# Two token halves of an HGRN head stepped together, each with its own PSUM bank

## The chip, the cores and the metric

The kernel runs on one core of a Trainium2 chip. The metric is device time in microseconds (us) of one execution. Engine names are those of the profile: PE is TensorE's matmul, DVE is VectorE, ACT is ScalarE, POOL is GpSimd, SP issues the DMAs. Each engine has its own list of instructions, and semaphores order the lists against each other.

## The reference, cut to what matters

One layer over 2048 tokens of width 1024. A combined projection gives the inputs of a pooling branch and of an HGRN branch (a gated linear recurrence of 8 heads, 128 wide). For each head the kernel must give

```
cum   = cumsum(logf)                       # within a chunk
score[t,s] = sum_d q[t,d] k[s,d] exp(cum[t,d]-cum[s,d])   for s <= t
o     = (q*exp(cum)) @ state + score @ v
state = exp(last) * state + (k*exp(last-cum))^T @ v
o     = rms_norm(o) * g * silu(gate)
```

followed by two output projections, gates and a final projection with a norm.

## The kernel before, in words

The 2048 tokens go through in two passes of 1024, and a pass in two halves of T = 512 tokens (t = 0, 1), a half being NT = 4 chunks of 128 or NB = 16 blocks of 32 tokens. After the V projection (`v_job`) a pass runs a stage over its 8 heads, then the projections `psA`, `psB` and `psy`.

In the head stage a head has three `quad`s (L470): "fq", "m" and "gp" (for the last head "gp" comes before "m"). A quad is seven products in Strassen's manner, each of 12 matmuls of 128x512 (`three`, L279), over four PSUM banks named `pa`, `pb`, `pe`, `pd` with the quad's name behind them (`pam`, `pem`, `pdm`, `pbm` belong to "m"). The order of the products in a quad is: `pa`; `pe`; `pa` again; `pb`; `pa` a third time; `pe` again; `pd`. Ahead of the last one stands `A.copy(d, a)` (L497), which ACT does from `pa` after its third product, while PE does `pe`; the `pd` product adds onto what the copy put there.

Between the products `tick()` (L961) gives each active generator one step. `hgrn` (L523) is such a generator, one for a head and a half. Its steps:

- `QR`, `K`, `TT`: operands built on ACT and DVE;
- four rounds of scores. Three of them, from `QR`, `X2` and `X8` (named so in the kernel's tiles), are 16 matmuls of 32 weight columns and 48 moving columns (`scores`, L597), into PSUM tile `psa`. After each, DVE writes the valid ones into `PT` with `copy_predicated` (`put`, L565: 2 after the first, 3 after each of the others) and updates `K` (`kup`, L555). The fourth round, called s64 below, has 16 matmuls of 32 or 64 columns (L648 to L653), and three ACT copies empty it;
- `pk` (transposes of K, copied to `KS` by ACT), `pd` (L671), the states `SC` (L676, DVE, four in a chain that starts from `S[h]`), `po` (16 profile records, L682), then `A.copy(S[h], ...)`, four squares `junk` on ACT (L688), two small operations on POOL (L689, L690), four scaled copies `on` on ACT (L693), and the transposes `pot` (L699).

Steps of the generator are apart by `yield`s, three between rounds of scores. Every fp32 matmul is two records in the profile, so a score round of 16 shows as x32.

`psa` is one tile of two banks, with 64 columns for each of the 16 blocks; a block's 32 rows stand in its own quarter of the partitions. Both halves of a head, and the next head, use it in turn. The second half's generator starts after the first of the two later quads, so seven ticks behind the first half. Four score buffers' worth of `qr` tiles are shared, and tag `px` has two banks for `pk`, `pd`, `po`, `pot`, `pw` and `xT`.

What stands where on an engine is not the order of the code: the tile framework places the instructions of every engine in a fixed list when the program is built, by its own costs, and the hardware keeps to these lists.

Of the kernel before, what the change touches and what calls it, by code (L numbers as in the profile page):

```python
# [8 lines left out]
F32 = mybir.dt.float32  # L9
# [9 lines left out]
P = 128  # L19
SEQ = 2048  # L20
D = 1024
T = 512
NT = T // P
NB = T // 32
# [8 lines left out]
LOOK = 4  # L33
MASK_W = P + 2 * 64 + 5 * NT * 64
NU = 76
KINDS = (("m", "gp"), ("gp", "m"))


# [30 lines left out]
def tile_block(ctx: ExitStack, tc: tile.TileContext, x, c, w_ada, b_ada, g_pre, g_post, w_in,  # L69
# [3 lines left out]
    V, A, G, PE, SP = nc.vector, nc.scalar, nc.gpsimd, nc.tensor, nc.sync  # L73
# [13 lines left out]
    ph = ctx.enter_context(tc.tile_pool(name="ph", bufs=1, space=bass.MemoryType.PSUM))  # L87
# [30 lines left out]
    r0 = 0  # L118
# [7 lines left out]
    mask = cst.tile([P, MASK_W], U8, name="mask")  # L126
# [43 lines left out]
    def split(src32, hi, lo):  # L170
        return A.copy(hi, src32), V.tensor_tensor(lo, src32, hi.bitcast(F32), op=SUB)  # L171
# [104 lines left out]
    def mm(o, l, r, start, stop):  # L276
        PE.matmul(o, lhsT=l, rhs=r, start=start, stop=stop, skip_group_check=True)  # L277
# [13 lines left out]
        return pj.tile([P, T], F32, tag="pj", name=name)  # L291


    psa = ph.tile([P, 2 * T], F32, tag="ph", name="psa")
    V.memset(psa, 0.0)
    s48 = psa.rearrange("p (b w) -> p b w", w=64)
    shv = cst.tile([P, 8], F32, name="shv")
    scv = cst.tile([P, 8], F32, name="scv")

# [28 lines left out]

    def ada_done(q):
        acc = accs.pop(q)  # L330
        v = psa[:, T + q * 4:T + q * 4 + 4]
        for j in range(4):
            it = PE.matmul(v[:, j:j + 1], lhsT=acc[:, j * P:(j + 1) * P], rhs=one, start=True, stop=True)
        sl = slice(q * 2, q * 2 + 2)
        V.tensor_tensor(shv[:, sl], v[:, 0:2], col("bsh")[:, sl], op=ADD)
        V.tensor_tensor(scv[:, sl], v[:, 2:4], col("bsc")[:, sl], op=ADD)
        iv = V.scalar_tensor_tensor(scv[:, sl], scv[:, sl], 1.0, col("gpre")[:, sl], op0=ADD, op1=MUL)
        return it, iv
# [171 lines left out]
    gens = [0]  # L510
# [12 lines left out]
    def hgrn(p, h, t, cx):  # L523
        n = f"{p}_{h}_{t}"
        F, Q = cx["F"].pop((h, t)), cx["Q"].pop((h, t))
# [4 lines left out]
        K = utile("K" + n)  # L530
# [5 lines left out]
        o = 0  # L536
        for hh in (1, 2, 4, 8, 16, 32, 64):
            w = T // (2 * hh)
            a = v2(Tb[hh], 2)
# [3 lines left out]
        yield  # L543

        pt = PT[gens[0] % 2]
        gens[0] += 1
        vh = cx["V"][h]

# [14 lines left out]
        moff = [0]  # L563

        def put(dst, src):  # L565
            shp = list(dst.shape[1:])
            w = int(np.prod(shp))
            if len(shp) == 2:
                w = w // NT
                m = mask[:, moff[0]:moff[0] + w].rearrange("p (a b) -> p a b", b=shp[1])  # L570
                m = m.unsqueeze(1).broadcast_to([P, NT, w // shp[1], shp[1]])
                dst = dst.rearrange("p (c a) b -> p c a b", c=NT)
                src = src.rearrange("p (c a) b -> p c a b", c=NT)
            else:
                m = mask[:, moff[0]:moff[0] + w]
                m = m.rearrange("p (a b c) -> p a b c", b=shp[1], c=shp[2])
                src = src.rearrange("p a (b c) -> p a b c", c=shp[2])
            V.copy_predicated(dst, m, src)  # L578
            moff[0] += w

        def blk(ap, b, hh):

# [14 lines left out]
        def scores(X):  # L597
            for i in range(NB):
                r0 = (i % 4) * 32
                mm(s48[r0:r0 + 32, i, 0:48], K[:, i * 32:(i + 1) * 32], X[:, i, :], True, True)  # L600

        def build(hh, b, w):
            X = qp.tile([P, b, 3 * w], F32, tag="qr", name=f"X{hh}_{n}")
# [16 lines left out]
        put(blk(ptf, NB, 1), s48[:, :, 32:48])  # L620
        kup(1)
        X = build(2, NB, 16)
        yield
        yield
        yield
        for hh in (2, 8):
            scores(X)
            put(blk(ptf, NB, hh), s48[:, :, 0:16])
            put(blk(ptf, NB, 2 * hh), s48[:, :, 16:32])
            put(blk(ptf, NB, 2 * hh), s48[:, :, 32:48])  # L630
            kup(hh)
            kup(2 * hh)
            if hh == 2:
                X = build(8, NB, 16)
            else:
                X = qp.tile([P, T], F32, tag="qr", name=f"X32_{n}")
                x32 = X[:, 0:T // 2].rearrange("p (b w) -> p b w", w=32)
                A.copy(x32, blk(Q, NB // 2, 32))
                qup(32)
                x64 = X[:, T // 2:T].rearrange("p (b w) -> p b w", w=64)  # L640
                tq = Tb[32].rearrange("p (a b) -> p a b", b=4)
                q64 = blk(Q, NT, 64)
                tt(x64, q64, bc(tq[:, :, 1], 64))
            yield
            yield
            yield
        s64 = psa.rearrange("p (c w) -> p c w", c=NT)
        for cc in range(NT):  # L648
            o = cc * P
            mm(s64[0:32, cc, 0:32], K[:, o:o + 32], x32[:, 2 * cc, :], True, True)  # L650
            mm(s64[32:64, cc, 64:128], K[:, o + 32:o + 64], Q[:, o + 64:o + P], True, True)
            mm(s64[64:96, cc, 0:32], K[:, o + 64:o + 96], x32[:, 2 * cc + 1, :], True, True)
            mm(s64[0:32, cc, 64:128], K[:, o:o + 32], x64[:, cc, :], True, True)  # L653
        A.copy(pt[0:64, :, 64:128], s64[0:64, :, 64:128])
        A.copy(pt[0:32, :, 32:64], s64[0:32, :, 0:32])
        A.copy(pt[64:96, :, 96:128], s64[64:96, :, 0:32])
        kup(32)
# [48 lines left out]
    def pv_got(p, g, t, u, cx):  # L706
        n = f"{p}_{g}_{t}"
        w = WINDOWS[g]
        PV = qp.tile([P, HALO + T], F32, tag="qr", name="PV" + n)
        A.copy(PV[:, 0:HALO], halo[:, g, :])  # L710
        A.copy(PV[:, HALO:], u)
        A.copy(halo[:, g, :], PV[:, T:T + HALO])
        cur, lo = PV, 0
        sh = 1
        while sh < w:
            nx = qp.tile([P, HALO + T], F32, tag="qr", name=f"W{sh}_{n}")
            lo += sh
            tt(nx[:, lo:], cur[:, lo:], cur[:, lo - sh:HALO + T - sh], op=ADD)
            cur = nx
            sh *= 2  # L720
        pm = utile("pm" + n)
        V.scalar_tensor_tensor(pm, cur[:, HALO:], 1.0 / w, PV[:, HALO:], op0=MUL, op1=SUB)
        if p == 0 and t == 0:
            e0 = pm[:, 0:HALO]
            tt(e0, cur[:, HALO:2 * HALO], icnt[:, g * HALO:(g + 1) * HALO])
            tt(e0, e0, PV[:, HALO:2 * HALO], op=SUB)
        pmh, pml = utile("pmh" + n, F32R), utile("pml" + n, F32R)
        split(pm, pmh, pml)
        yield
        pw = px.tile([P, T], F32, tag="px", name="pw" + n)  # L730
        wh, wl = pwh[:, g * P:(g + 1) * P], pwl[:, g * P:(g + 1) * P]
        mm(pw, wh, pmh, True, False)
        mm(pw, wh, pml, False, False)
        mm(pw, wl, pmh, False, True)
        pws = utile("pws" + n)
        A.activation(pws, pw, AF.Copy, scale=col("psc", g))
        cx["pw"][g, t] = pws
        yield
# [181 lines left out]
    for p in range(NPASS):  # L920
        cx = {k: {} for k in ("sm", "F", "Q", "G", "V", "pw", "Gd", "Pd", "Sd", "gP", "gG", "a", "mg", "x", "xc", "h32",
                              "mv", "y", "yss")}
# [13 lines left out]
    for p in range(NPASS):  # L936
# [4 lines left out]
        for h in range(NH):  # L941
            quad_items(("fq", h), O_F + h * P, O_Q + h * P, p == 0)
            for kind in KINDS[h == NH - 1]:
                if kind == "m":
# [14 lines left out]
    active = []  # L959
# [45 lines left out]
    for p in range(NPASS):  # L1005
        cx = cxs[p]
# [33 lines left out]
        for h in range(NH):  # L1040
            if h + 1 < NH:
                v_head(p, h + 1, cx)
            n = f"{p}_{h}"

            def fq(row, t, u):
                (f_got, q_got)[row](p, h, t, u, cx)

            def gp(row, t, u):
                if row == 1:
                    g_got(p, h, t, u, cx)  # L1050
                elif h % 2 == 1:
                    pg_got(p, h // 2, t, u, cx)
                else:
                    gen = pv_got(p, h // 2, t, u, cx)
                    next(gen)
                    active.append(gen)

            steps = []

            def tick_in():  # L1060
                tick()
                once(steps)

            quad("fq" + n, cx, fq, tick)
            active.append(hgrn(p, h, 0, cx))
            tick()
            for i, kind in enumerate(KINDS[h == NH - 1]):
                if kind == "gp":
                    quad("gp" + n, cx, gp, tick)
                else:  # L1070
                    if h == NH - 1:
                        steps += [lambda: None] * 2
                        steps += [lambda g=g: two_in("P", p, g, cx) for g in range(NG - 1)]
                    quad("m" + n, cx, lambda row, t, u: m_got(p, h, row, t, u, cx), tick_in)
                if i == 0:
                    active.append(hgrn(p, h, 1, cx))
                tick()
            if p + 1 < NPASS:
                x_stats(8 + h)
# [57 lines left out]
```

## Time and profile before

| | |
|---|---|
| median of 3 runs | 1841.29 us (1841.15 to 1844.52) |
| the profiled execution | 1843.0 us, span 1841.2 us |
| PE busy | 1797.7 us of the span |
| DVE busy | 1103.1 us |
| ACT busy | 807.5 us |
| head stage, first pass | from about 160 us to 700 us |
| head stage, second pass | from about 1030 us to 1600 us |

A busy time counts the union of an engine's instructions. In the chain of waits a row is a start, a duration, an engine, and a group of instructions that follow each other without a break; "x12" are profile records. Since the chain's pieces of PE follow each other without gaps, the duration of a piece is what it takes of PE's time, which is less than the duration of its instructions, as these overlap.

### The profile page before, as it was taken

The numbers are of one execution on the slowest core, as the hardware profiler recorded it, in microseconds if no ns is written. First come the engines' busy times: TensorE is split into PE (matmuls) and PEld (weight loads), VectorE is DVE, ScalarE is ACT, GpSimd is POOL, SyncE is SP. The second block draws the span as 40 slices with busy tenths as digits, with TensorE's granted clock in tenths as the row PEclk, the third lists the DMA queues.
The fourth block names the chain that finished last, engine by engine and source line by source line (L and its number), as shares of the span: only waits on it lengthen the run. The fifth ranks groups of instructions, "written<-read, shape, count | busy, mean of one in ns | idle before, by whom it ended". The sixth has DMA issues, their size and how long they took to land.

```text
span 1841.2 us, 31695 instructions
## 1 busy us (share of the span) xinstructions
PE 1797.7 (98%) x12053; PEld 1458.0 (79%) x12053; DVE 1103.1 (60%) x2329; ACT 807.5 (44%) x1863; POOL 71.1 (4%) x136
## 2 busy tenths in 40 slices
PE   5899999999999999999999999999999999999997
PEld 4788878888788777887788878878887888788886
DVE  7567887887888884565433255564555546633322
ACT  4655656656566562223322335445344345311111
POOL 1100000000000000000000000000000000000000
PEclk9999999999999999999999999999999999999999
DMA  8698677677676669987897756565665664794476
GB/s 299 225 317 289 213 280 251 218 267 254 232 264 240 233 220 327 361 287 261 285 323 241 249 184 198 199 206 180 207 210 162 223 210 161 241 354 144 142 256 235
DMA packets 236530, 444.19 MB, mean 241 GB/s; under 512 B 18989, under 2 KB 109786, under 8 KB 236378
## 3 DMA queue, kind: packets, MB, share of 16 engines
q1 hardware_dynamic: 236378, 442.17, 70.5%
q8 instruction: 95, 1.56, 0.4%
q14 instruction: 57, 0.47, 0.1%
HBM read 269.61 MB, written 172.49 MB: 240 GB/s over the span
## 4 chain that ended last, share of the span: by engine, by line
PE 90%; DMA 2%; DVE 2%; ACT 1%; issue 1%; SPq 0%; POOL 0%; POOLq 0%; DVEq 0%; ACTq 0%
PE psB L277 9%; PE psV L277 8%; PE psy L277 8%; PE pagp L277 7%; PE pafq L277 7%; PE pam L277 7%; PE pegp L277 5%; PE pefq L277 5%; PE psA L277 5%; PE pem L277 4%; PE psa L277 4%; PE po L277 3%; PE pbfq L277 3%; PE pbgp L277 2%; PE pdfq L277 2%; PE pdgp L277 2%
## 5 line engine op out<-in xcount | busy, mean ns | idle before, releaser
L171 DVE TENSOR_TENSOR whl<-wr,whl 128x512 fp32r<-128x512 f32 x210 | 144.8, 691 | 97.6 <-ACT whl L171 93.4
L578 DVE COPY_PREDICATED PT<-mask,psa 128x256 f32<-128x256 uint8 (+1 forms) x256 | 139.5, 545 | 60.9 <-PE psa L277 60.5
L171 ACT CAST whl<-wr 128x512 fp32r<-128x512 f32 x210 | 129.8, 621 | 103.5 <-issue 25.2
L277 PE MATMUL psV<-whl,hB 128*128 128x512 f32 x512 | 161.9, 398 | 1.4 <-ACT V L787 1.4
L277 PE MATMUL psy<-whl,mgh 128*128 128x512 f32 x512 | 160.2, 393 | 0.8 <-DVE y L391 0.7
L277 PE MATMUL psB<-Gh,whl 128*128 128x512 f32 x512 | 158.2, 389 | 0.0
L277 PEld LDWEIGHTS psV<-whl,hB 128*128 128x128 f32 x512 | 97.1, 192 | 21.4 <-ACT V L787 1.7
L277 PEld LDWEIGHTS psB<-Gh,whl 128*128 128x128 f32 x512 | 96.1, 188 | 20.8 <-issue 0.5
L277 PEld LDWEIGHTS psy<-whl,mgh 128*128 128x128 f32 x512 | 95.1, 188 | 21.9 <-DVE y L391 1.9
L277 PE MATMUL psV<-whl,lB 128*128 128x512 f32 x256 | 101.2, 397 | 0.0
L277 PE MATMUL psB<-Gl,whl 128*128 128x512 f32 x256 | 100.4, 392 | 0.0
L277 PE MATMUL psy<-whl,mgl 128*128 128x512 f32 x256 | 100.0, 390 | 0.0
L277 PE MATMUL pam<-hT,whl 128*128 128x512 f32 x256 | 85.9, 396 | 0.0
L277 PE MATMUL pagp<-hT,whl 128*128 128x512 f32 x256 | 85.9, 396 | 0.0
L277 PE MATMUL pafq<-hT,whl 128*128 128x512 f32 x256 | 84.3, 389 | 0.0
L277 PE MATMUL psA<-Ph,whl 128*128 128x512 f32 x256 | 83.3, 398 | 1.0 <-DMA Ph<-Pd 0.9
L277 PEld LDWEIGHTS psa<-X,K 128*32 128x32 f32 x2816 | 52.4, 109 | 39.3 <-issue 29.2
L391 DVE TENSOR_TENSOR K<-K,TT 128x256 f32<-128x256 f32 x192 | 81.3, 424 | 0.5
L171 ACT CAST mgh<-sm 128x512 fp32r<-128x512 f32 x32 | 19.7, 621 | 122.1 <-DVE sm L391 122.1
L277 PE MATMUL psa<-X,K 128*32 128x48 f32 (+2 forms) x2816 | 69.3, 209 | 1.4 <-ACT X L607 1.1
L391 DVE TENSOR_TENSOR y<-psy,gg 128x512 f32<-128x512 f32 x32 | 22.0, 689 | 73.9 <-ACT jy L893 73.8
L893 ACT ACTIVATE jy<-psy 128x512 bf16<-128x512 f32 x32 | 19.1, 597 | 92.2 <-PE psy L277 91.3
(358 smaller groups left out, 4320.1 us busy)
## 6 DMA issues: line engine op xcount, KB each, us to landing
wr<-in_w_in_dram SPq DMA_DIRECT2D x122, 256.0 KB, 3.5
whl<-scr_y SPq DMA_DIRECT2D x48, 512.0 KB, 3.9
sm<-Sd SPq DMA_DIRECT2D x64, 256.0 KB, 5.4
whl<-scr_v SPq DMA_DIRECT2D x32, 512.0 KB, 4.3
wa<-in_w_ada_dram SPq DMA_DIRECT2D x32, 256.0 KB, 5.4
x<-in_x_dram SPq DMA_DIRECT2D x32, 256.0 KB, 5.7
Vd<-V SPq DMA_DIRECT2D x32, 256.0 KB, 2.5
scr_v<-whl SPq DMA_DIRECT2D x16, 512.0 KB, 2.8
```

The lines of the kernel that those rows point to most:

```text
L171: return A.copy(hi, src32), V.tensor_tensor(lo, src32, hi.bitcast(F32), op=SUB)
L277: PE.matmul(o, lhsT=l, rhs=r, start=start, stop=stop, skip_group_check=True)
L391: return (e or V).tensor_tensor(o, a, b, op=op)
L578: V.copy_predicated(dst, m, src)
L893: A.activation(jy, pss[tk], AF.Square, scale=1.0 / 32, accum_out=rs[:, nn:nn + 1])
```

## The change

`psa` becomes two tiles of one bank each (`psa0`, `psa1`), and a generator takes the one that goes with its `PT`. Inside a bank a chunk has 128 columns, and the four blocks of a chunk write the same columns, each in its quarter of the partitions. `put` reads the source with a broadcast over these four, so it writes the same number of elements as before, under the same mask. The s64 round uses columns 32 to 96 where it used 64 to 128. The `memset` of `psa` is gone.

Both halves of a head enter `active` together after "fq", so their steps come in the same tick, and five `yield`s (`GAP`) stand between rounds where there were three. The pooling generator `pv_got` has one `yield` more.

One thing changes in what is computed: in the step of `pd` both halves now write their `SC` before the copy into `S[h]` that follows the first half's `po`. The second half's chain of states therefore starts from `S[h]` as it was ahead of the first half; before, it started from the state after it.

```
-    psa = ph.tile([P, 2 * T], F32, tag="ph", name="psa")
-    V.memset(psa, 0.0)
-    s48 = psa.rearrange("p (b w) -> p b w", w=64)
+    psa = [ph.tile([P, T], F32, tag=f"ph{i}", name=f"psa{i}") for i in range(2)]
...
         pt = PT[gens[0] % 2]
+        s48 = psa[gens[0] % 2].rearrange("p (c w) -> p c w", c=NT)
         gens[0] += 1
...
         def put(dst, src):
+            w = src.shape[2]
+            if len(dst.shape) == 3:
+                m = mask[:, moff[0]:moff[0] + 4 * w].rearrange("p (a b) -> p a b", b=w)
+                moff[0] += 4 * w
+                shp = [P, NT, 4, w]
+                V.copy_predicated(dst.rearrange("p (c a) b -> p c a b", c=NT), m.unsqueeze(1).broadcast_to(shp),
+                                  src.unsqueeze(2).broadcast_to(shp))
+                return
+            a, b = dst.shape[2:]
+            m = mask[:, moff[0]:moff[0] + NB * w].rearrange("p (c q a b) -> p c q a b", c=NT, q=4, b=b)
+            moff[0] += NB * w
+            V.copy_predicated(dst.rearrange("p (c q) a b -> p c q a b", c=NT), m,
+                              src.rearrange("p c (a b) -> p c a b", b=b).unsqueeze(2)
+                              .broadcast_to([P, NT, 4, a, b]))
...
-                mm(s48[r0:r0 + 32, i, 0:48], K[:, i * 32:(i + 1) * 32], X[:, i, :], True, True)
+                mm(s48[r0:r0 + 32, i // 4, 0:48], K[:, i * 32:(i + 1) * 32], X[:, i, :], True, True)
...
-        yield
-        yield
-        yield
+        for _ in range(GAP):
+            yield
...
-            active.append(hgrn(p, h, 0, cx))
+            active.extend(hgrn(p, h, t, cx) for t in range(2))
...
-                if i == 0:
-                    active.append(hgrn(p, h, 1, cx))
```

**The lists.** Over the whole program PE's list has 2048 score matmuls before and after. Before they stand in 151 unbroken runs, now in 95. What follows a run is a group of transposes (`pk`, `pot`) 24 times before and 2 times now, and else (127 and 93 times) a product or another 128-column group. Groups of `pk`, `pd`, `po`, `pot` followed by a product are 129 before and 67 now.

PE's list where head 4 of the second pass has its `X8` round. The names are tile names with pass, head and half; `h` and `l` tiles are the two parts of the activations, `whl` the weights. Before, the first half's round, in two pieces, of which this is the first:

```order
L277 MATMUL pagp1_4_13973<-lB111_3_9596,whl386_13849 128x512
L277 MATMUL pagp1_4_13973<-hB111_3_9595,whl386_13849 128x512
L277 MATMUL psa_116<-X8_1_4_0_13948,K1_4_0_13733 32x48 x2
L277 MATMUL pegp1_4_13990<-hT11_0_10443,whl387_13893 128x512
L277 MATMUL pegp1_4_13990<-lT11_0_10444,whl387_13893 128x512
```

Now:

```order
L278 MATMUL pdgp1_4_14115<-lT41_3_10643,whl392_14085 128x512
L278 MATMUL pdgp1_4_14115<-hT41_3_10642,whl392_14085 128x512
L278 MATMUL psa0_116<-X8_1_4_0_14036,K1_4_0_13685 32x48 x16
L278 MATMUL psa1_117<-X8_1_4_1_14063,K1_4_1_13692 32x48 x16
L278 MATMUL pafq1_5_14247<-hB111_0_9275,whl393_14116 128x512
L278 MATMUL pafq1_5_14247<-lB111_0_9276,whl393_14116 128x512
```

Four pieces of the two halves' rounds (2, 14, 9 and 7 matmuls) have become one run of 32 at the end of the quad. In 11 of the 14 heads that are followed by another in their pass, the first one to three matmuls of the s64 round (both halves have 32) now stand one product behind this run, behind the first `pafq` of the next head, and the others behind the third `pafq`.

ACT's list in quad "m" of head 4 of the second pass, around the copy `pdm<-pam`. Before, with the second half of head 3:

```order
L497 COPY pdm1_4_13848<-pam1_4_13736 128x512
L684 COPY S3_128<-SC1_3_1_13799 128x128
L756 ACTIVATE c22m1_4_13768<-c22m1_4_13768 128x512
L688 ACTIVATE junk0_1_3_1_13878,ss1_3_1_13877<-po1_3_1_13867 128x128
L688 ACTIVATE junk1_1_3_1_13880,ss1_3_1_13877<-po1_3_1_13867 128x128
L688 ACTIVATE junk2_1_3_1_13882,ss1_3_1_13877<-po1_3_1_13867 128x128
L688 ACTIVATE junk3_1_3_1_13884,ss1_3_1_13877<-po1_3_1_13867 128x128
L693 ACTIVATE on1_3_1_13888<-po1_3_1_13867,ss1_3_1_13877 128x128 x4
```

Now, with both halves of head 3 (the squares of its first half stand just ahead of these rows):

```order
L692 ACTIVATE on1_3_0_13823<-po1_3_0_13802,ss1_3_0_13812 128x128 x4
L687 ACTIVATE junk0_1_3_1_13839,ss1_3_1_13838<-po1_3_1_13828 128x128
L605 COPY X8_1_4_1_14063<-sq1_4_1_13587 128x16x16
L687 ACTIVATE junk1_1_3_1_13841,ss1_3_1_13838<-po1_3_1_13828 128x128
L709 COPY PV1_2_0_14099<-halo_145 128x16
L687 ACTIVATE junk2_1_3_1_13843,ss1_3_1_13838<-po1_3_1_13828 128x128
L687 ACTIVATE junk3_1_3_1_13845,ss1_3_1_13838<-po1_3_1_13828 128x128
L692 ACTIVATE on1_3_1_13849<-po1_3_1_13828,ss1_3_1_13838 128x128 x4
L608 COPY X8_1_4_1_14063<-sq1_4_1_13587 128x16x16
L496 COPY pdm1_4_13904<-pam1_4_13695 128x512
```

The copy stood ahead of the half's squares, and now stands behind the squares and scaled copies of both halves. On PE's list the two `po` have moved with them. Before, the second half's `po` stood behind the third `pam`, and `pem` and `pdm` came next. Now both `po` stand ahead of the third `pam`, in the order `pbm`, `po` of half 0, `po` of half 1, both `QR` rounds of the new head, `pam`, `pem`, `pdm`, `pot` of half 0, `pot` of half 1. It is so in all 14 quads that hold a `po` pair (six "m" and one "gp" a pass). The last head's `po` pair falls into the `psA` stage.

More of the change, by code (lines that the diff above doesn't have):

```diff
@@ L35 @@
 NU = 76
+GAP = 5
 KINDS = (("m", "gp"), ("gp", "m"))
@@ L330, in ada_done @@
         acc = accs.pop(q)
-        v = psa[:, T + q * 4:T + q * 4 + 4]
+        v = psa[0][:, q * 4:q * 4 + 4]
         for j in range(4):
@@ L565, in put @@
         def put(dst, src):
[L566 to L579, printed above, removed]
+            w = src.shape[2]
[12 more added lines that the diff above has]
+                              .broadcast_to([P, NT, 4, a, b]))
         def blk(ap, b, hh):
@@ L643, in hgrn @@
                 tt(x64, q64, bc(tq[:, :, 1], 64))
[L644 to L647, printed above, removed]
+            for _ in range(GAP):
+                yield
+        s64 = s48
         for cc in range(NT):
@@ L650, in hgrn @@
             mm(s64[0:32, cc, 0:32], K[:, o:o + 32], x32[:, 2 * cc, :], True, True)
-            mm(s64[32:64, cc, 64:128], K[:, o + 32:o + 64], Q[:, o + 64:o + P], True, True)
+            mm(s64[32:64, cc, 32:96], K[:, o + 32:o + 64], Q[:, o + 64:o + P], True, True)
             mm(s64[64:96, cc, 0:32], K[:, o + 64:o + 96], x32[:, 2 * cc + 1, :], True, True)
-            mm(s64[0:32, cc, 64:128], K[:, o:o + 32], x64[:, cc, :], True, True)
-        A.copy(pt[0:64, :, 64:128], s64[0:64, :, 64:128])
+            mm(s64[0:32, cc, 32:96], K[:, o:o + 32], x64[:, cc, :], True, True)
+        A.copy(pt[0:64, :, 64:128], s64[0:64, :, 32:96])
         A.copy(pt[0:32, :, 32:64], s64[0:32, :, 0:32])
@@ L728, in pv_got @@
         split(pm, pmh, pml)
+        yield
         yield
```

## The prediction

> **What bounds the kernel now.** First the page's busy line and its chain by engine; then the busy time in two stretches of the head stage, one of each pass.
>
> ```profile
> PE 1797.7 (98%) x12053; PEld 1458.0 (79%) x12053; DVE 1103.1 (60%) x2329; ACT 807.5 (44%) x1863; POOL 71.1 (4%) x136
> PE 90%; DMA 2%; DVE 2%; ACT 1%; issue 1%; SPq 0%; POOL 0%; POOLq 0%; DVEq 0%; ACTq 0%
> 230.00:300.00 70.00, 70.00 (x565) 56.75 (x565) 57.66 (x128) 43.87 (x104) 3.28 (x6) 1.00 0.75 262
> 1170.00:1240.00 70.00, 70.00 (x566) 56.38 (x565) 36.92 (x90) 31.41 (x81) 2.40 (x4) 1.00 0.62 195
> ```
>
> In the last two rows the second and third numbers are the stretch and PE's busy time: 70.00 of 70. DVE (57.66 and 36.92) and ACT (43.87 and 31.41) have room, and the clock is 1.00. So in the head stage the time is the length of PE's list. Whatever shortens that list counts in full, and any new wait on PE counts in full too. The chain of waits, a stretch at a time, gives what each piece of the list takes:
>
> ```profile
> 229.97 2.77 PE pbm L277 x12
> 232.75 0.48 PE psa L277 x32
> 233.22 2.94 PE pam L277 x12
> 236.16 1.78 PE po L277 x16
> 237.95 2.76 PE pem L277 x12
> 240.71 2.72 PE pdm L277 x12
> 243.43 0.48 PE psa L277 x32
> 243.90 0.59 PE pot L699 x4
> 244.49 2.75 PE pagp L277 x12
> 247.25 0.21 PE psa L277 x4
> 247.46 2.95 PE pegp L277 x12
> 250.41 2.72 PE pagp L277 x12
> 253.12 0.47 PE psa L277 x28
> 253.59 2.94 PE pbgp L277 x12
> 288.15 2.95 PE pdfq L277 x12
> 291.10 0.44 PE pot L699 x4
> ```
>
> Here "x32" is one whole round of 16 score matmuls. A product costs 2.72 behind another product (`pdm`), about 2.755 behind 128-column groups (`pem`, `pagp`), and 2.94 behind scores (`pam`). `pot` costs 0.59 behind scores and 0.44 behind a product. Scores of 4 records cost 0.21, of 32 records 0.48. So a score run costs about 0.17 to start and 0.01 a record. The work is cheap; the borders of a run are not.
>
> **The change part by part: borders removed.** By the counts of the two lists, 151 score runs become 95. Each of the 56 runs that vanish saves its 0.17: 9.5 us. Runs followed by a product or another 128-column group fall from 127 to 93, at 2.94 − 2.72 = 0.22: 7.5. Runs followed by transposes fall from 24 to 2, at 0.59 − 0.44 = 0.15: 3.3. Groups of transposes, `pd` and `po` followed by a product fall from 129 to 67, at 0.035: 2.2. Sum **−22.5 us**, all on PE, which nothing hides. The doubt is whether two rounds of 16 back to back, in different banks, are one run to the hardware: if the start is paid again where the half changes, 9.5 is lost and −13 is left. I take the whole, since within a run each matmul already goes to another quarter of the partitions than the one ahead of it, and costs 0.01 a record so.
>
> **A new wait for the copy `pdm<-pam`.** In the 14 quads with a `po` pair this copy now stands behind both halves' squares and `on` on ACT's list, and PE's last product needs it. ACT's own rows, and POOL's:
>
> ```profile
> 305.21 0.42 ACT L615 COPY QR<-sq 128x256 f32<-128x256 f32 x1
> 307.32 0.57 ACT L497 COPY pdm<-pam 128x512 f32<-128x512 f32 x1 [1.58 <-PE pam L277]
> 307.80 0.30 ACT L684 COPY S<-SC 128x128 f32<-128x128 f32 x1
> 308.00 0.62 ACT L171 CAST whl<-wr88s 128x512 fp32r<-128x512 f32 x1
> 309.19 0.26 ACT L688 ACTIVATE junk<-po 128x128 bf16<-128x128 f32 x1
> 310.54 0.19 ACT L688 ACTIVATION_READ_ACCUMULATOR junk<-po 128x1 f32 x1
> 311.10 1.01 POOL L391 TENSOR_TENSOR ss<-ss,mh 128x4 f32<-128x4 f32 x1
> 312.14 1.14 ACT L693 ACTIVATE on<-po,ss 128x128 f32<-128x128 f32 x4 [1.40 <-POOL ss L391]
> 313.16 0.64 ACT L171 CAST whl<-wr 128x512 fp32r<-128x512 f32 x1
> ```
>
> Four squares with their read-outs take 309.19 to 310.73, 1.54. Then ACT stands still 1.41 until POOL's power is done. The four `on` take 312.14 to 313.16, 1.02. During the pause a cast with nothing to wait for stood next on ACT's list, and did not run. (The Trainium skill, "PSUM — Partial Sum Buffer", section "Engine vs sequencer instructions", calls the queues of ScalarE, VectorE and GpSimdE strict FIFO; that row agrees. If ACT could take the copy first, the sum below would lack its second term.)
>
> Let 0 be the end of the second `po`; the first ended 1.78 earlier (its row). ACT: state copy 0.20 and squares 1.54 end at 0; the pause to 1.4; `on` to 2.4; four squares of the second half and an `X8` copy (0.4, as the `QR` row of the same shape) to 4.35; the pause to 5.75, since POOL's work cannot start ahead of the squares; `on` to 6.8; one more `X8` copy to 7.2; `pdm<-pam` (0.57) to 7.75. PE: both `QR` rounds, 0.17 + 64 × 0.011 = 0.86; `pam` 2.94 to 3.8; `pem` 2.72 to 6.52. PE then waits about 1.25. In the first pass a cast stands among these rows and part of it fills a pause; I take 1.35 there. So 14 × 1.3 = **+18.2 us**. The bounds: nothing, if the copies of `X8` and the squares overlap so that the chain ends by 6.5; 2.2 a quad if a cast of 0.62 and a second late reader fall in: 31 us.
>
> Behind the late copy stand on ACT the next head's copies and the read of `pdm`. These are needed a product later, so I cost nothing more; if that cover is missing, their 0.4 to 0.6 a quad is within the upper bound.
>
> **The last head.** Its `po` pair falls into `psA`, and there `pot` of the second half stands only one product (2.76), scores and `pot` behind the pair: 3.9, while the second `on` is done at about 6.2 by the same chain. That is +2.3 in the first pass. The two `kup`s and `pk` close to the s64 round add about 1. One row goes away:
>
> ```profile
> PE psa L277 <- DVE PT L578: 1.2, 2, 0.9
> PE pst L138 <- DMA rows<-in_hgrn_norm_g_dram: 4.6, 1, 4.6
> L295 DVE MEMSET psa<- x1: 912/912/912, 1.0 to 1.0; 128x1024 f32 x1
> ```
>
> PE waited 1.2 in all for a bank that DVE still read; with a bank for each half this should end: −1.2. Net **+2**. The memset of 0.912 at 1.0 us into the span lies under the 4.6 that PE waits there for DMA rows: nothing.
>
> **Scores ahead of the evacuation.** In 11 heads one to three s64 matmuls stand one product behind the `X8` run. They need three `put`s and two `kup`s:
>
> ```profile
> 1134.00 0.75 DVE L578 COPY_PREDICATED PT<-mask,psa 128x512 f32<-128x512 uint8 x1 [0.81 <-PE psa L277]
> 1144.67 0.73 DVE L578 COPY_PREDICATED PT<-mask,psa 128x256 f32<-128x256 uint8 x1 [2.53 <-PE psa L277]
> 1145.21 0.45 DVE L391 TENSOR_TENSOR K<-K,TT 128x256 f32<-128x256 f32 x1
> 1145.58 0.41 DVE L578 COPY_PREDICATED PT<-mask,psa 128x256 f32<-128x256 uint8 x1
> 1160.63 0.68 DVE L171 TENSOR_TENSOR Pl<-spg,Ph 128x512 fp32r<-128x512 f32 x1
> L578 DVE COPY_PREDICATED PT<-mask,psa 128x256 f32<-128x256 uint8 (+1 forms) x256 | 139.5, 545 | 60.9 <-PE psa L277 60.5
> ```
>
> With starts about 0.33 apart, five such steps end near 1.8, with two of DVE's 512-wide rows (0.68) between them near 3.2. PE is there 0.35 + 2.94 = 3.3 after the first half's matmuls. So nothing to 1 us a head; I take **+1 us** in all.
>
> `put` now reads a broadcast source. It writes as many elements under the same mask, so I keep 545 ns. Bounds: nothing, or each of 192 narrow `put`s rising from 0.41 to 0.73, 192 × 0.3 = 58 us of DVE time, which DVE's idle time holds in the second pass but hardly in the first, where 57.66 of 70 is taken. The closest row is the one of the same element count, 0.41.
>
> **Sum.** The profiled execution took 1843.0, 1.7 above the median of 1841.29. 1843.0 − 22.5 + 18.2 + 2 + 1 = 1841.7, less 1.7: **1840.0 us**. A measurement of this kernel can tell about 0.2%, 3.7 us, from no change.
>
> **Rivals.** *The copy is in time* (0.35). What decides is 1.2 us in a chain of 9.5 us that I put together from rows seen in other places; ACT is only 44% busy, and if POOL's power overlaps the squares of the other half, or the copy's place is less hard than I think, the stall goes: 1843.0 − 1.7 − 22.5 + 3 = 1822; with half the stall 1831. Against it: the two pauses of 1.41 are in series, as the second squares must precede the second power.
>
> *DVE's evacuation becomes the bound* (0.15, slower). Both halves' `put`s and `kup`s now come in one burst, up to 12 rows of 0.35 to 0.75, about 5 us, and the next round or `pk` waits for the last. Five ticks (some 14 us) stand between rounds of the same head, but only one or two products between `X8` and s64. At 1 us for each of 16 heads the time is 1856, at 0.7 to 2 us 1851 to 1872; it decides from 3.3 us of burst. For it speaks 57.66 of 70 in the first pass; against it the 60.5 us in which DVE waited for `psa`, so DVE is mostly early. The Trainium skill, "TensorEngine Tiling (Array Packing)", section "PSUM Bottleneck", warns of this: small tiles speed up TensorE and not the emptying of PSUM, whose copies may become the bottleneck. In the row of 60.5 us it is the other way round so far.
>
> *Two halves are not one run* (0.13, slower). Then 56 × 0.17 = 9.5 us of the gain are not there, and the waits stay: 1849.5. That the merged run does less than it looks would show as x64 at 1.03 in place of 0.86. The same page, section "Key Properties", speaks against it: changing the tiling mode, not merely the tile, drains TensorE, and both halves are in one mode; by it the sum stays.
>
> **How the numbers follow.** My forecast, stall and gain nearly equal, has 0.37, with a range of its own of 1836 to 1845, a little of which (0.05) is faster than 1837.6. Faster by over 0.2%: 0.05 and the first rival, 0.40. Within 0.2%: 0.32. Slower by over 0.2%: the other two rivals, 0.28. The range goes from 1822, the stall gone, to 1856, the burst at 1 us a head; some 0.2 lie outside.
>
> **What would show it.** Right: in the chain of the changed kernel score pieces x64 of about 0.86; PE's busy time some 22 us lower; and among the waits PE for `pdm` (and `pdgp`) released by ACT's copy, 14 times about 1.3 us. If these rows are missing, the second term is wrong and the time is near 1822. `PE psa` released by DVE's `K` or `PT` for more than 10 us would show the burst, and a mean of `put` well above 545 ns the broadcast's cost. PE waiting for ACT's `on` ahead of `pot` in `psA` shows the last head's term. The forecast is wrong as a whole if PE's busy time does not fall.

## The result and the profile after

The changed kernel is slower: 1854.64 us (median of 4 runs, 1851.48 to 1855.46) against 1842.08 for the kernel before (4 runs). The ratio is 1.0063, with a 95% interval of 1.0046 to 1.0080. The forecast was 1840.0, no change that could be told.

The profiled execution of the changed kernel took 1851.48, with a span of 1849.7. First the page's busy line and its chain by engine, then two stretches of the head stage as they were shown of the kernel before (stretch, its length, then busy time of PE, PEld, DVE, ACT, POOL, clock, DMA share, GB/s):

```profile
PE 1782.6 (96%) x12053; PEld 1456.7 (79%) x12053; DVE 1089.1 (59%) x2328; ACT 799.9 (43%) x1863; POOL 80.0 (4%) x136
PE 79%; ACT 6%; DMA 3%; DVE 3%; POOL 2%; issue 2%; SPq 1%; POOLq 0%; DVEq 0%; ACTq 0%
230.00:300.00 70.00, 67.78 (x555) 55.33 (x554) 55.90 (x119) 41.89 (x102) 3.89 (x6) 1.00 0.72 250
1170.00:1240.00 70.00, 68.85 (x567) 56.46 (x565) 36.87 (x91) 30.70 (x80) 2.60 (x4) 1.00 0.62 204
```

PE's busy time fell from 1797.7 to 1782.6, 15.1 us. What PE stood still rose from 1841.2 − 1797.7 = 43.5 to 1849.7 − 1782.6 = 67.1, 23.6 us. The head stage is no longer full: PE has 67.78 and 68.85 of 70 where it had 70.00, and ACT and POOL now take 8% of the chain where they had 1%.

What PE waited for in the changed kernel, by the view of waits (total, times, longest). The last row is that of PE's weight loads:

```profile
PE pdm L278 <- ACT pdm L496: 14.4, 12, 1.3
...
PE pdgp L278 <- ACT pdgp L496: 3.2, 2, 2.1
PE pot L698 <- ACT on L692: 2.2, 1, 2.2
PE psa L278 <- DVE PT L572: 2.1, 3, 1.0
PE psA L278 <- DVE sm L390: 1.7, 2, 1.5
PE psA L278 <- DMA Ph<-Pd: 1.7, 2, 1.2
PE pbfq L278 <- DMA whl<-scr_('fq', 0)_3_1388: 1.7, 1, 1.7
PE pk L663 <- DVE K L390: 1.0, 2, 0.6
...
PEld pdm L278 <- ACT pdm L496: 19.5, 12, 1.7
```

The kernel before had no row for `pdm`, `pdgp`, `pot` or `pk`. The forecast's wait for the copy is there, in all 14 quads, 14.4 + 3.2 = 17.6 us. The chain of waits of one such quad of the first pass reads as the prediction laid it out:

```profile
232.33 0.54 POOL ss L688
...
232.95 1.08 POOL ss L390
...
234.06 1.14 ACT on L692 x4
235.20 0.26 ACT junk L687 x2
...
236.98 1.20 POOL ss L390
...
238.20 1.14 ACT on L692 x4
239.35 0.50 ACT pdm L496
...
239.89 3.02 PE pdm L278 x12
242.91 0.87 PE pot L698 x8
```

ACT and POOL take turns, two sets of squares, two powers, two sets of `on`, and the copy comes last. The second half's squares needed only its `po`, which had ended at 232.17, but they stand behind the first half's `on` on ACT's list and began at 235.07. The copy ended 7.7 behind the `po` pair (the forecast was 7.75), and PE was there at 6.5 (6.52).

The row after the copy was not in the forecast: `pdm` takes 3.02 behind the wait, where a product behind a product takes 2.72. The other 13 quads have 3.02 to 3.07. That is 0.30 a quad, 4.2 us over 14; it is called the slow start below. PE's weight loads waited with it (19.5 against 14.4 us for `pdm`).

The other part of the change is right there as well: both halves' rounds run as one.

```profile
1170.55 2.72 PE pdgp L278 x12
1173.27 0.82 PE psa L278 x64
1174.09 2.94 PE pafq L278 x12
```

64 records took 0.82 (the forecast was 0.86, and 1.03 if each half were a run of its own).

### The profile page after: what moved, and what is told of

Its sections match the earlier page's. It is cut to its first block, busy times and chain, and to the rows that moved or that the text cites. A ratio compares the mean times of both kernels' runs of the same rounds, so it can differ in the third digit from the quotient of the medians.

```text
span 1849.7 us, 31713 instructions
## 1 busy us (share of the span) xinstructions
PE 1782.6 (96%) x12053; PEld 1456.7 (79%) x12053; DVE 1089.1 (59%) x2328; ACT 799.9 (43%) x1863; POOL 80.0 (4%) x136
## 4 chain that ended last, share of the span: by engine, by line
PE 79%; ACT 6%; DMA 3%; DVE 3%; POOL 2%; issue 2%; SPq 1%; POOLq 0%; DVEq 0%; ACTq 0%
PE psB L278 9%; PE psV L278 8%; PE psy L278 8%; PE pafq L278 6%; PE pagp L278 6%; PE pam L278 5%; PE pefq L278 5%; PE psA L278 4%; PE pegp L278 4%; PE pem L278 3%; PE psa L278 3%; PE pbfq L278 2%; PE pbm L278 2%; PE pdfq L278 2%; PE pdm L278 2%; PE pbgp L278 2%
## 5 line engine op out<-in xcount | busy, mean ns | idle before, releaser
L578 DVE COPY_PREDICATED PT<-mask,psa 128x256 f32<-128x256 uint8 x160 | 86.1, 548 | 51.5 <-PE psa L278 51.5
L278 PEld LDWEIGHTS psy<-whl,mgh 128*128 128x128 f32 x512 | 95.0, 188 | 22.5 <-DMA whl<-scr_y 1.7
L278 PE MATMUL psa<-X,K 128*32 128x48 f32 (+2 forms) x2816 | 61.0, 208 | 2.1 <-DVE PT L572 2.1
L572 DVE COPY_PREDICATED PT<-mask,psa 128x256 f32<-128x256 uint8 (+1 forms) x96 | 51.9, 541 | 18.3 <-PE psa L278 18.3
```

Of the source, the lines that this page charges most:

```text
L572: V.copy_predicated(dst.rearrange("p (c a) b -> p c a b", c=NT), m.unsqueeze(1).broadcast_to(shp), src.unsqueeze(2).broadcast_to(shp))
L578: V.copy_predicated(dst.rearrange("p (c q) a b -> p c q a b", c=NT), m, src.rearrange("p c (a b) -> p c a b", b=b).unsqueeze(2) .broadcast ...
```

## The experiments

All times stand against runs of the kernel before on the same chip. The theory (A in the expectations): PE's own work did get shorter, and the loss is ACT's chain of both halves' norm, which is longer than PE's work between `po` and what PE needs of ACT next. The rivals: a burst of `put` and `kup` on DVE, the price of the broadcast, or the merged runs themselves.

### The second half's po one step later

```
             sts.append(nxt)
         yield
         yield
+        for _ in range(1 * t):
+            yield
         po = px.tile([P, NT, P], F32, tag="px", name="po" + n)
```

> The second half of a head waits one step longer ahead of its `po`, all else as in the change (that half still takes `S[h]` from ahead of the first). On PE's list `po` of half 1 then stands behind the third `pam`, and on ACT's list `pdm<-pam` behind the first half's chain only. Theory A (ACT's chain of both halves' squares, POOL pauses and scaled copies makes the `pdm` copy late, and PE pays the wait and a slow start behind it): the waits for `pdm` and `pdgp` (14.4 + 3.2 us) and 14 starts of 0.30 go, and 15 more borders cost 0.7: 1854.6 - 21 = about 1834, PE's idle time lower by 17 to 18. Theory B (the burst of `put` and `kup` on DVE, or the broadcast source of `put`, costs it): the time stays above 1850. Theory C (the chain is merely late for its next reader): waits show up at `pot` instead, and the time is 1840 to 1848.

One thing the expectation left out: half 1's `po` now reads `PT` after the next head's first round has begun to write it, so its scores are in part the next head's. The work is the same, and `po` gets a small wait for `PT`.

Measured: 1835.79, ratio 0.9957 (0.9946 to 0.9969). PE's waits name `pdm` and `pdgp` no more, and the new one is small. First the busy line, then that wait:

```profile
PE 1781.4 (97%) x12053; PEld 1456.5 (80%) x12053; DVE 1090.0 (60%) x2328; ACT 797.8 (44%) x1863; POOL 74.3 (4%) x136
PE po L278 <- DVE PT L578: 2.8, 8, 0.4
```

The span fell by 18.7 us, nearly all of it PE's idle time (67.1 to 49.6). Its busy time fell by 1.2 only: the slow starts of `pdm` and `pdgp` are gone, but each `po` that waits for `PT` has one of its own, 2.05 for its 16 records where the others take 1.78. Moving one group on PE's list by one product, with the score runs left at 95, turned the loss into a gain. Theory A named 1834.

### The same, with the states chained

```
-        sts = [S[h]]
+        sts = [S[h] if t == 0 else cx["st"].pop(h)]
...
+        if t == 0:
+            cx.setdefault("st", {})[h] = sts[NT]
...
-        A.copy(S[h], sts[NT])
+        if t == 1:
+            A.copy(S[h], sts[NT])
```

> As the stagger, and the second half's chain of states starts from the last `SC` of the first half, as the kernel before has it; the first half's copy into `S[h]` is gone. Theory A: the same time as the stagger within 2 us (about 1834 to 1836): DVE's four dependent steps of 0.34 come after four more, 1.4 later, and `po` of half 1 stands four products behind `pd`. Should the chain of eight steps be late, PE waits for `SC` in up to 16 heads, 0.5 each: 1842.

Half 1's `po` stands as in the run above, and reads `PT` as late. Measured: 1833.97, ratio 0.9953 (0.9940 to 0.9965), the same as without the chained states. That the changed kernel's two halves both start from `S[h]` therefore hid no cost: eight dependent steps on DVE were early enough, here with `po` one step later and in the reordered chain below with `po` in its place.

### POOL's power left out

```
         G.tensor_scalar(ss, ss, 1.0 / P, EPS, op0=MUL, op1=ADD)
-        tt(ss, ss, mh[:, 0:NT], op=ALU.pow, e=G)
```

> The change, without POOL's power of `ss` (so the norm's scale is left out of what is computed: `on` is scaled by the mean square). PE's and ACT's lists keep their order. Theory A: each of the two pauses in ACT's chain is shorter by about 1.0, the chain ends near 5.75 where PE comes at 6.5, so the waits for `pdm` and `pdgp` go and the slow starts with them: about 1833. Theory B: POOL's power is no part of it, 1853 to 1856.

Measured: 1825.65, ratio 0.9908 (0.9893 to 0.9922), 29 us below the changed kernel with the same places on PE's and ACT's lists. The busy line, and the chain where the changed kernel's was shown:

```profile
PE 1778.5 (98%) x12053; PEld 1457.5 (80%) x12053; DVE 1089.8 (60%) x2328; ACT 799.1 (44%) x1863; POOL 43.7 (2%) x104
231.94 0.82 PE psa L278 x64
232.76 2.95 PE pam L278 x12
235.71 2.72 PE pem L278 x12
238.43 2.73 PE pdm L278 x12
241.16 0.87 PE pot L697 x8
```

No wait, and `pdm` takes 2.73. The length of ACT's chain is what stalls PE, and two instructions of about 1 us in each of these quads, on an engine that is 4% busy, decide it. The gain is larger than the 21 us expected. Between the two spans, 1849.7 and 1822.3, lie 27.4: PE's busy time is 4.1 lower (the slow starts), and its idle time, 1822.3 − 1778.5 = 43.8, is 23.3 lower and about that of the kernel before (43.5). The last head's wait for `on` ahead of `pot` fell from 2.2 to 0.2 and the waits for `PT` (2.1) went too, and the expectation had not counted them.

### The copy made by DVE

```
         prod(a, "T3", False)
-        A.copy(d, a)
+        V.tensor_copy(d, a)
```

> The change, with the copy `pdm<-pam` made by DVE in place of ACT; PE's order is the same. Theory A: the copy no longer stands behind the two chains; in the second pass (DVE busy 37 of 70) all waits go, in the first (56 of 70) a copy may come behind one or two rows of 0.69 and still be in time, since `pem` takes 2.72: 1832 to 1840. Theory B (DVE is the tight engine): no faster than 1852, waits of PE for DVE of 10 us or more. Theory C: the ACT chain's other readers (`pot`, the `X8` copies) stall PE instead, 1840 to 1850.

Measured: 1829.02, ratio 0.9924 (0.9912 to 0.9936).

```profile
PE 1780.7 (97%) x12053; PEld 1458.8 (80%) x12053; DVE 1114.4 (61%) x2376; ACT 774.9 (42%) x1815; POOL 76.1 (4%) x136
PE pot L698 <- ACT on L692: 2.2, 1, 2.2
PE pdgp L278 <- DVE pdgp L496: 0.9, 1, 0.9
```

DVE was given 25 us more work and the kernel got 26 us faster. That rules out DVE as the bound. Of 14 waits one is left (0.9), and the last head's `pot` keeps its 2.2.

### The two banks alone

The kernel before with two tiles, stacked columns and the new `put`; the halves seven steps apart, three steps between rounds.

> The kernel before with the change's two banks, stacked columns and `put` alone: the halves seven steps apart, three steps between rounds. The lists have the same 151 score runs. Theory A: a bank for each half by itself is worth the wait of 1.2 us that it ends, and the broadcast source costs nothing: 1840 to 1843. If the broadcast cost 0.3 a `put`, DVE's busy time would be 58 us up and the time 1845 or more.

Measured: 1841.59 over 11 runs, ratio 0.9995 (0.9986 to 1.0004): no difference. DVE's busy time is 1102.3, against 1103.1. A cost of the broadcast does not show; in the changed kernel the groups of `put` read

```profile
L578 DVE COPY_PREDICATED PT<-mask,psa 128x256 f32<-128x256 uint8 x160 | 86.1, 548 | 51.5 <-PE psa L278 51.5
L572 DVE COPY_PREDICATED PT<-mask,psa 128x256 f32<-128x256 uint8 (+1 forms) x96 | 51.9, 541 | 18.3 <-PE psa L278 18.3
```

with means of 548 and 541 ns where there was one of 545, and DVE waited 51.5 + 18.3 us for scores. The Trainium skill's warning that emptying PSUM may become the bottleneck ("TensorEngine Tiling (Array Packing)", section "PSUM Bottleneck") did not come true here: it is mostly DVE that waits, and PE waited 2.1 us for `PT`.

### Lockstep on one tile

The kernel before with the halves in lockstep and five steps, on its one `psa` tile.

> The two halves in lockstep, five steps between rounds, but both on the one `psa` tile of the kernel before, 64 columns a block. The second half's scores wait for the first half's `put`s, so products stand between them: 146 score runs, 54.1 us of borders (54.3 before). Theory A: no gain from merged runs, and the late `pdm` copy stays with its wait of 1.25 and slow start of 0.30 in up to 14 quads: 1842.6 + 10 to 22, about 1860; a few us more where PE waits for `put`.

Measured: 1861.46, ratio 1.0106 (1.0093 to 1.0119).

```profile
PE 1802.3 (97%) x12053; PEld 1457.5 (78%) x12053; DVE 1098.6 (59%) x2329; ACT 800.6 (43%) x1863; POOL 80.9 (4%) x136
PE pdm L278 <- ACT pdm L498: 9.3, 12, 0.8
PE pdgp L278 <- ACT pdgp L498: 2.4, 2, 1.3
```

This took the two halves of the theory apart. Without banks of their own the runs do not merge: PE's busy time is 1802.3, against 1797.7 before, and 14 slow starts of 0.30 are 4.2 of the difference. The late copy stays. So the bank for each half is what makes lockstep pay on PE, and lockstep with five steps is what makes the copy late.

### Fewer steps between rounds

`GAP = 4` and `GAP = 3` in place of 5, nothing else. Each moves the `po` pair to another place on PE's list.

> The change with four steps between score rounds in place of five. The score runs stay as merged (96 for 95), but the `po` pair moves to the end of the next head's fq quad, ahead of its first `pam`; the next copy PE needs from ACT behind it is `pbm<-pam`, four products later (about 9 us), in place of two. Theory A (the place of the pair ahead of a copy that is needed 6.5 us later is the whole loss): waits of PE for ACT's copies of 1 us at most in all, PE's own work as in the change without the slow starts (1786 to 1787 us by starts), 1842.6 - 17 = about 1826. Theory B (bursts on DVE from lockstep): no better than 1840.

> The change with the three steps of the kernel before between score rounds. Score runs fall to 81, and the `po` pair stands behind the third `pafq`, with `pdfq<-pafq` ahead of the squares on ACT's list. Theory A: by the borders of its list (31.4 us of them, 54.3 before) 1842.6 - 23 = 1820, and `pot` of half 1 may wait 0.5 in 14 quads, 1827. Theory B (DVE's burst): with `X8` two products behind `X2`, DVE has both halves' `put`s and `kup`s, some 5 us, in 5.7 us; if late by 1 us a head the time is 1836, and PE waits for DVE's `K` or `PT`.

Both missed. Four steps: 1849.00, ratio 1.0036 (1.0024 to 1.0048). Three steps: 1845.10 over 12 runs, ratio 1.0017 (1.0009 to 1.0025). The late copy is gone from both (a wait of 0.2 for `pdgp` is left with three steps), but the same chain is late for another reader. PE's waits with four steps, then with three:

```profile
PE pot L698 <- ACT on L692: 11.7, 17, 1.3
PE psa L278 <- DVE PT L578: 5.8, 6, 1.2
```

```profile
PE pot L698 <- ACT on L692: 8.9, 14, 0.7
PE psa L278 <- DVE PT L578: 8.5, 7, 1.7
```

With three steps a quad looks so on PE (start, duration, line, operation, and the idle time in brackets):

```profile
1128.34 0.60 PE L698 MATMUL pot<-ident,on 128*128 128x128 f32 x4
1129.59 0.66 PE L698 MATMUL pot<-ident,on 128*128 128x128 f32 x4 [0.65 <-ACT on L692]
1130.00 0.48 PE L278 MATMUL pam<-hB,whl 128*128 128x512 f32 x1
```

`pot` of half 0 is on time, that of half 1 waits 0.65 for `on`; from 1128.34 to 1130.00 the eight records take 1.66, where the run without the power has 0.79 from the first `pot` to the product behind it (240.99 to 241.78). I had ruled out such a wait from the place of the copy alone, with no regard for `pot`, and put it at 0.5 a quad at the most in the expectation of three steps.

### Both halves' squares first

This run puts ACT's chain in another order: all eight squares, then the two sets of `on`, so that POOL works on half 0 while ACT squares half 1. The states are chained as above, and `po` stays in its place.

```
-            A.activation(junk[:, 0:P], po[:, cc, :], AF.Square, accum_out=ss[:, cc:cc + 1])
+            it = A.activation(junk[:, 0:P], po[:, cc, :], AF.Square, accum_out=ss[:, cc:cc + 1])
+        cx.setdefault("jk", {})[h] = it
...
         tt(ss, ss, mh[:, 0:NT], op=ALU.pow, e=G)
+        yield
         on = utile("on" + n)
-        for cc in range(NT):
-            A.activation(on[:, cc * P:(cc + 1) * P], po[:, cc, :], AF.Copy, scale=ss[:, cc:cc + 1])
-        yield
+        with after(cx["jk"][h]):
+            for cc in range(NT):
+                A.activation(on[:, cc * P:(cc + 1) * P], po[:, cc, :], AF.Copy, scale=ss[:, cc:cc + 1])
         yield
         yield
```

`after` holds half 0's `on` behind the last square of half 1 on ACT's list.

> The change with ACT's chain put in another order: the squares of both halves first, then both sets of `on`, so that the first half's POOL pause lies under the second half's squares; the second half's states start from the first half's last `SC`, as in the kernel before. Score runs and places on PE's list as in the change. Theory A (the chain's length is what stalls PE): from the end of the second `po`, squares and an `X8` copy to 1.95, pause to 3.35, both `on` to 4.4 at the earliest, copies to 5.4, ahead of PE's 6.5: waits for `pdm` and `pdgp` go, 1825 to 1829. Were the number of ACT's instructions and not the pauses the cause, at most 5 us of the 12 would come back: 1848 or more.

> The same reordered chain with three steps between score rounds. In the run with three steps alone PE waited 8.9 for `on` ahead of `pot`, and the four transposes of half 1 then ran at the pace of the four `on` (1.70 for eight, 0.79 without), some 1.5 us in each of 14 quads. Theory A: with `on` of half 1 done 4.4 to 5.4 behind the `po` pair and PE there at 6.5 these go, 1845.1 - 21 = 1824; the waits for `PT` (8.5) stay, and the time is 1822 to 1830. If `pot` is slow for another reason, 1840 or more.

With five steps 1825.11, ratio 0.9907 (0.9891 to 0.9924); with three 1823.18, ratio 0.9895 (0.9881 to 0.9910). Both are faster than either kernel, and all of the norm is computed. Five steps, the chain of waits and ACT's rows for the same stretch:

```profile
1121.52 3.57 PE po L278 x32
1125.09 0.82 PE psa L278 x64
1125.91 2.95 PE pam L278 x12
1128.86 2.72 PE pem L278 x12
1131.58 2.73 PE pdm L278 x12
```

```profile
1126.97 1.15 ACT L698 ACTIVATE on<-po,ss 128x128 f32<-128x128 f32 x4
1128.49 1.14 ACT L698 ACTIVATE on<-po,ss 128x128 f32<-128x128 f32 x4 [0.38 <-POOL ss L390]
1129.51 0.42 ACT L608 COPY X<-sq 128x256 f32<-128x256 f32 x1
1129.81 0.61 ACT L496 COPY pdm<-pam 128x512 f32<-128x512 f32 x1
```

Half 0's `on` has no pause ahead of it, half 1's has 0.38 (1.40 in the row of the kernel before). The copy ends at 1130.42, 5.3 behind the end of `po`, and PE comes for it at 1131.58. The waits for `pdm`, `pdgp` and the last head's `pot` are gone, and ACT has only the 16 state copies less, which were worth nothing in the staggered pair above. With three steps the busy line and what is left of the waits for `PT` are

```profile
PE 1775.2 (97%) x12053; PEld 1455.7 (80%) x12053; DVE 1085.2 (60%) x2328; ACT 804.0 (44%) x1847; POOL 70.4 (4%) x136
PE psa L278 <- DVE PT L578: 0.7, 2, 0.4
```

and the `pot` wait is gone too. The waits for `PT`, which I had expected to stay at 8.5, fell to 0.7: most of them hung on the same chain, it seems, since besides the chained states nothing else was changed; by which steps was not traced. Between the two runs with three steps, spans 1841.4 and 1822.2, lie 19.2 us: 15.3 of idle time of PE (62.3 and 47.0) and 3.9 of busy time (1779.1 and 1775.2), the same two shares, wait and slow start, as with five steps.

## Why the prediction was wrong

The mechanisms of the forecast were there, with their signs. The sum was 14.6 us too low, in these terms, all but the last from PE's busy and idle time of the profiled executions:

| term | forecast | measured | from |
|---|---|---|---|
| borders removed | −22.5 | −19.2 | busy 1797.7 to 1778.5, in the run without the power |
| slow start behind a wait | not there | +4.1 | busy 1782.6 − 1778.5; 14 × 0.30 is 4.2 |
| wait for the copy | +18.2 | +17.6 | 14.4 + 3.2 |
| last head, early scores | +3 | +4.1 | 2.2 + 1.0 + 2.1, less 1.2 |
| other waits, small ones | 0 | +1.9 | idle +23.6, less the two rows of waits above |
| profiled execution against the median | −1.7 | +3.2 | 1851.48 and 1854.64 |

**The sum of the borders, "−22.5 us, all on PE", was mis-sized: −19.2.** Part of it is a counting slip: the runs "followed by a product or another 128-column group" fell by 34, but those followed by a product, to which the 0.22 belongs, fell in the trace from 118 to 91, by 27. That is 1.5 us. Most of the rest is the start of a run, taken as 0.17: two runs x32 took 2 × 0.48 = 0.96 and one x64 takes 0.82, so a merged run saves 0.14. The traces say the same where each piece of PE's work is taken from the end of the piece before it to its own end, without idle time, and added up, for the kernel before and the run without the power:

| PE's pieces | before | without the power | difference | forecast |
|---|---|---|---|---|
| score runs | 81.6 | 74.1 | −7.5, 0.13 a run | −9.5 |
| `pk`, `pd`, `po`, `pot` | 118.0 | 114.4 | −3.6 | −3.3 |
| products of the quads | 944.2 | 936.3 | −7.9 | −7.5 − 2.2 = −9.7 |

The two banks alone, with the 151 runs of the kernel before, have 81.8, 117.9 and 944.3, so these sums hold to a few tenths. The changed kernel's quads have 940.5, the 4.2 of the slow starts above the run without the power. The step that was called doubtful, whether two halves are one run, was right (0.82 for x64).

**"PE then waits about 1.25 ... 14 × 1.3" was right in its size and left out what the wait does to the product behind it.** The product takes 3.02 to 3.07 in place of 2.72, in all 14 quads; in the run without the power it takes 2.73. The forecast put nothing for it. The price could have been read in the kernel before, in the one product of its quads that stands behind a wait (0.7 us, for a DMA): `1040.51 3.02 PE pbfq L277 x12`.

**"I cost nothing more" for what stands behind the late copy held.** With five steps the reader behind it (`pot`, 0.87 right behind `pdm` in the chain) was on time. With three and four steps, where the copy is not late, `pot` was the reader that the chain kept waiting.

**"1841.7, less 1.7" took more from one execution than it bears.** The 1.7 was the distance to a median of three. Sets of 11 and 23 executions of the kernel before, beside the experiments, had medians of 1842.60 and 1842.72, so its profiled execution, 1843.0, was near the middle. Four executions of the changed kernel lie between 1851.48 and 1855.46, and the profiled one was the fastest; what the others spent more was not traced. The profiled execution was forecast as 1841.7 and took 1851.48: 9.8 too low by the upper five rows. The rest of the 14.6 is this term, 4.9.

**The rivals.** *The copy is in time* did not happen, yet its number, 1822, is close to what the reordered chain gave (1825.11, and 1823.18 with fewer score runs still): the gain that the change holds was sized well, the condition for it failed. *DVE's evacuation becomes the bound* fell with the copy made by DVE: more work there, and a faster kernel. The measured 1854.64 lies near the 1856 of this rival and inside the range, but that is luck: the upper end stood for a burst on DVE, and what came was ACT's chain. *Two halves are not one run* fell with the 0.82.

The forecast lay so near to nothing because two terms of about 20 us nearly cancelled. About a fifth of either is as wide as the band of 3.7 us. The borders came out 3.3 smaller and slow starts of 4.1 were left out: either moves 1840.0 from below the kernel before to above it, and both together leave the band.

## What to carry to other kernels

When two streams are put in lockstep to make runs on one engine longer, the work that follows each stream on another engine also doubles up in one place: add up that chain, pauses for a third engine included, and compare it with the time until each reader needs it, not only the first. A stall on a full PE costs its length and a slow start behind it. A chain that alternates between two engines is shortened by interleaving the streams (all first steps, then all second ones), which here was worth 29.5 us (1854.64 to 1825.11).

## What the runs showed of the hardware that was not expected

A wait on PE made the product behind it 0.30 us longer (3.02 and 2.72), and the rows show no dependence on its length: waits of 0.7, 1.2 and 2.1 us gave 3.02 each. The weight load waited with the product (19.5 us for PEld, 14.4 for PE): in the quad at 239.89 the first load starts at 239.88, 0.01 ahead of its matmul, where in the run without the power it starts at 238.04, 0.22 ahead. The Trainium skill says that a single matmul cannot hide its drain while a stream of them does ("TensorE: Matmul & The Clock Gate", section "Step-by-step: what each phase is for"); these rows agree that a start from standstill has a price of its own, and no run here tells drain from weight load.

Stacking four blocks' scores on the same PSUM columns, each in its quarter of the partitions, and reading them through a broadcast cost nothing that could be measured in the run with the two banks alone (ratio 0.9995, 0.9986 to 1.0004).
